# Small steps of the mixer wait in the planner for free PSUM buffers; z products share the stream's two buffers

## The chip, the cores and the metric

The kernel runs on one core of a Trainium2 chip. The metric is the device time of one execution in microseconds (us); less is better. Before the change three runs took 814.40, 811.92 and 809.09 us, a median of 811.92 us.

## What is computed

The reference is two transformer blocks in float32 on 256 tokens of width 1024. Cut to what matters here:

```
x = first_block(x)                      # attention + convolutional FFN + RMSNorm
h = layer_norm(concat([meta(16 tokens), x]))        # 272 tokens
proj = h @ w_in                         # dn q,k,v | dn z | b,a | sb q,k,v | gates
q,k,v = silu(conv4(dn_qkv)); q,k normalised;  beta, g from b, a
o_dn = gated_delta_rule(q,k,v,beta,g)   # chunks of 16, 128, 128 tokens; needs (I + A)^-1 per chunk
o_dn = rms_norm(o_dn) * silu(dn_z)
o_sb = stick_breaking_attention(sq, sk, sv)         # 8 heads
mix  = (gate0 * (o_dn @ w_branch_dn) + gate1 * (o_sb @ w_branch_sb)) @ w_out
h = layer_norm(ALPHA*h + mix);  h = layer_norm(ALPHA*h + mixture_of_32_experts(h))
```

The change lies in the mixer, the part between the first layer norm and `mix`.

## The kernel before

**The stream.** All products with large weights form one list, the stream, in a fixed order. A weight slab comes by DMA into a ring of three, ScalarE rounds a part of it (`high`, the tiles hiA and hiB) and VectorE takes the remainder (`lower`, loA and loB), so that a float32 product is three fast products. A unit of the stream is half a tile of 128 output columns, 12 products; two units fill one PSUM tile (`fm_tile`), and after the second one `emit` reads the tile. In the mixer the order is sk, dn k, v, q, sq (queries of the stick-breaking heads), sv, z (the argument of silu(dn_z)), the eight gate tiles of branch 0, then the branch products `br`, which may start only when the whole mixer is done (gate "br0", opened behind `drive(... "o2" in done and "sb3" in done)`).

**The threads.** All other work is in generators. `dn_prep` makes, for each of three chunks, the decay matrix (tile drow), the Gram matrices (gram, kq) and transposed v and q (vtp, qtp). `inverse_thread` inverts I + A by doubling: six levels, each a product Y, copies to SBUF, products Z and ZT, and subtractions; the first level is the tile xt, the last joins two halves (YL, ZL). `state_thread` then carries the state through the chunks (KS, w, Su, QS, PW), and `o_thread` normalises, transposes (otp) and writes `od`. Beside that `sb_pair` runs four pairs of heads: scores (two tiles sz), a masked add on VectorE, exponentials on ScalarE, running sums on VectorE, transposes (swm, swt), the product with the values (sav) and two reads of it into `os`.

**The order of the work.** The instructions of each engine run in the order in which the program issues them; `drive` fixes that order when the program is built. It keeps a modelled clock for each engine (`Queue`, `TensorQueue`, `Clock`), takes a thread step when its time has come, and feeds stream products when TensorE has had too few columns lately (`owed`, 1300 wanted in the mixer) or when no thread is ready. `Clock.run` lets TensorE's modelled clock run on when a step has to wait for a buffer, but the step is issued at that place all the same.

**PSUM.** It has eight buffers of 128x512 float32: four with the tag acc, two g and two a. Stream tiles take g, but the four z tiles take acc before the change; most thread steps take acc; svt, sz, swm and sav take a. A thread step takes its buffer (`acc_tile`, `a_tile`) and issues its products at once; if that buffer is still to be read by VectorE or ScalarE, TensorE stands at these products, and all that was issued behind them stands too.

`z_emit` holds its tile long: it reads it with the first exponential on ScalarE and again with a multiplication on VectorE after two more ScalarE steps:

```
A.activation(z, p, AF.Exp, scale=-1.0)
A.activation(z, z, AF.Ln, bias=1.0)
A.activation(z, z, AF.Exp, scale=-1.0)
V.tensor_mul(z, z, p)
```

Of the kernel before, what the change touches and what calls it, by code (L numbers as in the profile page):

```python
# [20 lines left out]
N_META = 16  # L21
# [26 lines left out]
WANT = 1000.0  # L48
MIX_WANT = 1300.0

TURN = 0.13
LNS = 1.0


# [8 lines left out]
class Clock:  # L63
# [49 lines left out]
    def turn(self, tag, bufs, tile):  # L113

        names = self.tags.setdefault(tag, [])
        if len(names) == bufs:
            old = min(names, key=lambda n: self.last.get(n, 0))
            names.remove(old)
            self.used[tile.name] = [((0, 128, 0, 1 << 20), at, by) for _, at, by in self.used.get(old, ())]
        names.append(tile.name)  # L120
        return tile


# [64 lines left out]
class TensorQueue:  # L188
# [23 lines left out]
    def matmul(self, out, w, x, pair=False, **k):  # L212

        n, m, r = size(x), size(w), x.shape[0]
        if x.dtype == F32:
            half = 2 if pair or (r <= 64 and m <= 64) else 1
            self.run(max(n, m) / 600 / half + 0.01, 2 * n * r / 128 / half, [out], [w, x])
        else:
            self.run(n / 2400 + (0.0115 if x.dtype == F32R else 0.0025), n * r / 128, [out], [w, x])
        return self.engine.matmul(out, w, x, **k)  # L220
# [119 lines left out]
def build(tc, I, out):  # L340
# [35 lines left out]
    with ExitStack() as ctx:  # L376
# [30 lines left out]

        def a_tile(name):
            return clock.turn("a", 2, ps.tile([128, 512], F32, tag="a", bufs=2, name=name))


        def rsqrt(v, n, rows=128):
# [17 lines left out]
        def finish(flag):  # L430
            done[flag] = clock.end
# [583 lines left out]
        def win_tiles(c0, n0, emit, name, gate=None, room=None, mk=g_tile):  # L1015
            sl_ = load_cols(win, c0, name)
            for c in range(2):
                fm_tile(sl_, c, XH, mk, n0, lambda p, c=c: emit(c, p), (gate, None), room=room)
# [40 lines left out]
        def sv_emit(f, p):  # L1059
            n = d2_turns.take()  # L1060
            sv = M["d2"]("sv")[:, :3].rearrange("p a b -> p (a b)")[:, :NT]
            A.copy(sv, p)

            def turn():
                yield
                p = a_tile("svt")
                T.transpose(p[:16, 0:128], sv[:, 0:16], ident)
                T.transpose(p[:, 128:256], sv[:, 16:144], ident)
                T.transpose(p[:, 256:384], sv[:, 144:272], ident)
                d2_turns.give(n)  # L1070
                V.tensor_copy(M["svm"][:, f * 128:f * 128 + 128], p[:16, 0:128])
                V.tensor_copy(M["svt"][:, :, f * 128:f * 128 + 128], p[:, 128:384].rearrange("p (a b) -> p a b", a=2))
                finish("sv%d" % f)

            spawn(turn())

        def z_emit(f, p):
            z = M["z"][:, f]
# [4 lines that stand above are left out]
            finish("z%d" % f)  # L1083
# [38 lines left out]
        for s in range(2):  # L1122
            win_tiles(3080 + s * 256, 0, lambda c, p, s=s: sv_emit(2 * s + c, p), "wsv", None, d2_turns.free)
        for s in range(2):
            win_tiles(1536 + s * 256, N_META, lambda c, p, s=s: z_emit(2 * s + c, p), "wz", "mix2", None, acc_tile)
        br = {}

        def merge(f, m, n):
# [421 lines left out]
        def dn_prep_thread():  # L1550

            p = acc_tile("dcp")
            for ci, (t0, C) in enumerate(CH):
                T.matmul(p[:C, ci * 4:ci * 4 + 4], ut[:C, :C], gg[:C, ci], start=True, stop=True)
            V.memset(FN, 1.0)
            V.tensor_copy(fd[:16, 0], p[:16, 0:4])
            V.tensor_copy(fd[:, 1:3], p[:, 4:12].rearrange("p (c h) -> p c h", c=2))
            yield from wait("k")
            for ci, (t0, C) in enumerate(CH):
                X_ = DNC[ci]  # L1560
                yield from room(d2_turns)
                n = d2_turns.take()
                sq = d2("dsq")
                pk = acc_tile("ktp")
                for h in range(4):
                    T.transpose(pk[:C, h * 128:(h + 1) * 128], kdT[:, h, t0:t0 + C], ident)
                if ci < 2:
                    X_["ktok"] = (dm if ci else iv).tile([128 if ci else 16, 4, 128], F32, name="ktok%d" % ci)
                for h in range(4):
                    A.activation(sq[:C, h], v4(pk)[:C, h], AF.Square, accum_out=fk[:C, ci, h:h + 1])  # L1570
                if ci < 2:
                    A.copy(X_["ktok"][:C], v4(pk)[:C])
                yield
                d2_turns.give(n)
                yield
            for n in "vq":
                yield from wait(n)
            A.preload_act_table_set("natural_log_exp_and_others")
            A.activation(fe, fd, AF.Exp)
            V.tensor_scalar(fk, fk, 1e-6, None, op0=OP.add)  # L1580
            V.reciprocal(fb_, fk)
            V.tensor_mul(fb_, fb_, beta)
            V.tensor_scalar(fn_, fe, -1.0, None, op0=OP.mult)
            rk = rsqrt_log(fk.rearrange("p c h -> p (c h)"), 12)
            V.tensor_mul(fk, fk, rk.rearrange("p (c h) -> p c h", c=3))
            for ci in (1, 2, 0):
                spawn(dn_prep(ci))
            spawn(inverse_thread())
            spawn(state_thread())
            yield  # L1590

        def dn_prep(ci):
# [4 lines left out]
            yield from room(d2_turns)  # L1597
            nE = d2_turns.take()
            E = d2("E")[:, :, :C]
            pr = acc_tile("drow")  # L1600
            for h in range(4):
                T.transpose(pr[:, h * C:(h + 1) * C], fd[:C, ci, h:h + 1].to_broadcast([C, 128]), ident[:C, :C])
# [4 lines left out]
            yield  # L1607
            A.activation(E[:C], E[:C], AF.Exp)
            yield
            p = acc_tile("gram")  # L1610
            for h in range(4):
                T.matmul(p[:C, h * C:(h + 1) * C], kdT[:, h, sl], kdT[:, h, sl], start=True, stop=True)
# [15 lines left out]
                    V.scalar_tensor_tensor(X_["PT"][:C, h], p2[:C, h * C:(h + 1) * C], fb_[:C, ci, h:h + 1], E[:C, h], op0=OP.mult, op1=OP.mult)  # L1628
            d2_turns.give(nE)
            yield  # L1630
            pv = acc_tile("vtp")
            for h in range(4):
                T.transpose(pv[:C, h * 128:(h + 1) * 128], M["raw3"][2][:, h, sl], ident)
# [47 lines left out]
        def inverse_thread():  # L1681
# [8 lines left out]
            for g in B:  # L1690
                g.mask(0)
            yield
            P = []
            for g in B:
                P.append(g.psum("xt"))
# [4 lines left out]
                V.tensor_sub(g.x, g.bc(identc), p)  # L1700
            yield
            for l in range(1, 6):
                P = []
                for g in B:
                    P.append(g.psum("Y"))
                    g.each(P[-1], g.am, lambda b, i, g=g: g.x[b, i])
                for g, p in zip(B, P):
# [5 lines left out]
                    if l < g.levels - 1:  # L1713
                        g.mask(l + 1)
                yield
                P = []
                for g in B:
                    if g.n == 8:
# [17 lines left out]
                    finish("inv0")  # L1736
                yield
            g = B[0]
            p = g.psum("YL")
            for i in range(8):  # L1740
                T.matmul(p[hi, i], DNC[1 + i // 4]["AT"][lo, i % 4, hi], g.x[lo, i], start=True, stop=True)
            A.copy(g.y[hi, 0:4], p[hi, 0:4])
            V.tensor_copy(g.y[hi, 4:8], p[hi, 4:8])
            yield
            p = g.psum("ZL")
            for i in range(8):
                T.matmul(p[lo, i], g.y[hi, i], XT[hi, i // 4, i % 4, hi], start=True, stop=True)
# [6 lines left out]
        def state_thread():  # L1754
            Sst = None
            for ci, (t0, C) in enumerate(CH):
# [4 lines left out]
                if Sst is None:  # L1761
                    R = X_["vp"]
                else:
                    yield from room(d2_turns)
                    nR = d2_turns.take()
                    R = d2("R")
                    p = acc_tile("KS")
                    for h in range(4):
                        T.matmul(p[:C, h * 128:(h + 1) * 128], kdT[:, h, sl], Sst[:, h], start=True, stop=True)
                    for h in range(4):  # L1770
                        V.scalar_tensor_tensor(R[:C, h], p[:C, h * 128:(h + 1) * 128], fn_[:C, ci, h:h + 1], X_["vp"][:C, h],
                                               op0=OP.mult, op1=OP.add)
                    yield
                yield from room(d2_turns)
                nw = d2_turns.take()
                w = d2("w")
                p = acc_tile("w")
                for h in range(4):
                    T.matmul(p[:C, h * 128:(h + 1) * 128], X_["XT"][:C, h], R[:C, h], start=True, stop=True)
# [5 lines left out]
                Sold = Sst  # L1785
                yield
                if ci < 2:
                    p = acc_tile("Su")
                    for h in range(4):
                        T.matmul(p[:, h * 128:(h + 1) * 128], X_["ktok"][:C, h], w[:C, h], start=True, stop=True)  # L1790
# [9 lines left out]
                    Sst = Sn  # L1800
                if ci > 0:
                    qs = X_["vp"]
                    p = acc_tile("QS")
                    for h in range(4):
                        T.matmul(p[:, h * 128:(h + 1) * 128], qdT[:, h, sl], Sold[:, h], start=True, stop=True)
# [30 lines left out]
        def o_thread(ci, qs, so_):  # L1836
# [5 lines left out]
            for n in range(4):  # L1842
                yield from wait("z%d" % n)
            og = qs
            p = acc_tile("otp")
            for h in range(4):
                T.transpose(p[:, h * 128:(h + 1) * 128], qs[:, h], ident)
# [21 lines left out]
        def sb_pair(pr):  # L1869
# [3 lines left out]
            nl = l_turns.take()  # L1873
            z = sw.tile([128, 2, 416], F32, "z", "z%d" % (nz % 2))
            l = sw.tile([128, 2, 416], F32, "l", "l")
            P = [a_tile("sz") for hh in range(2)]
            for a in range(2):
                for hh in range(2):
# [19 lines left out]
            yield  # L1898
            yield from room(w_turns, pr)
            nw = w_turns.take()  # L1900
            pm = a_tile("swm")
            PT = []
            for hh in range(2):
# [10 lines left out]
            V.tensor_copy(wm, pm[:16])  # L1914
            z_turns.give(nz)
            yield
            av = a_tile("sav")
            for c in range(3):
                for hh in range(2):
# [8 lines left out]
            w_turns.give(nw)  # L1928
            oh, ol = M["o"][1]
            A.copy(oh[:, pr], av[:, :S])  # L1930
            yield
            V.tensor_sub(ol[:, pr], av[:, :S], oh[:, pr].bitcast(F32))
            finish("sb%d" % pr)

        stream.open("win")
# [599 lines left out]
```

## Time and profile before

| | |
|---|---|
| median of 3 runs | 811.92 us |
| profiled execution | 807.77 us, span 806.0 us |
| TensorE matmuls busy | 764.5 us (95%) |
| VectorE busy | 503.7 us (62%) |
| ScalarE busy | 399.4 us (50%) |
| mean granted TensorE clock | 0.974 |
| DMA | 187.15 MB, mean 232 GB/s |

Times in rows are microseconds from the start of the span. PE is TensorE (PEld its weight loads), DVE VectorE, ACT ScalarE, POOL GpSimd. A busy PE says that some product was under way, not that it ran at full rate: the granted clock (PEclk) stands beside it, 1.00 for 2.4 GHz and 0.50 for 1.2 GHz, and a value between is a mean over both. The name before the arrow is the tile written, those behind it the tiles read; some small tiles are cut out of one large one and all are called cut. In brackets stands the idle time before an instruction and what ended it.

### The profile page before, as it was taken

Reading aid. Unit: us, or ns where it says so; the run is one execution under the profiler, and the core shown is the slowest. Engines: PE = TensorE matmul, PEld = TensorE weight load, DVE = VectorE, ACT = ScalarE, POOL = GpSimd, SP = SyncE. Lnnn points to the kernel's source line nnn. Section 1 sums busy time; section 2 is a strip of 40 time slices with the busy share of each in tenths; the row PEclk is TensorE's granted clock in tenths of the full one; section 3 lists DMA queues with packets and bytes.
Section 4 is the critical chain, followed back from the end, with each engine's and each line's share of the span. In section 5 each row is a group of like instructions: output and inputs, shape, how many; then the busy total and the mean of one; then the engine's idle time right before and its main releaser. Section 6 shows DMA issues by size and latency. Waiting matters only on the chain. (4 is left out here: it accounts for less than half of the span.)

```text
span 806.0 us, 17077 instructions
## 1 busy us (share of the span) xinstructions
PE 764.5 (95%) x6839; PEld 650.9 (81%) x6839; DVE 503.7 (62%) x1268; ACT 399.4 (50%) x861; POOL 46.8 (6%) x74
## 2 busy tenths in 40 slices
PE   8999999999999999999899889999999999998984
PEld 7989998999999999889898679999876555545442
DVE  6786667997888888899878638655663211130104
ACT  7555566775566666676535455745343111212201
POOL 0000001000000000343000000001300000000001
PEclk9999999999999999999999979999999999988998
DMA  8534553465455464385511104996789999999992
GB/s 299 184 110 153 164 160 105 159 216 202 158 179 188 158 207 158 106 305 166 157 54 55 54 1 157 387 403 241 267 326 365 420 425 426 420 426 423 424 390 88
DMA packets 93971, 187.15 MB, mean 232 GB/s; under 512 B 10490, under 2 KB 71219, under 8 KB 82499
## 3 DMA queue, kind: packets, MB, share of 16 engines
q1 hardware_dynamic: 93731, 185.78, 62.8%
q8 instruction: 54, 0.88, 0.4%
q10 hardware_dynamic: 160, 0.27, 0.1%
q14 instruction: 26, 0.21, 0.1%
HBM read 184.99 MB, written 1.05 MB: 231 GB/s over the span
## 5 line engine op out<-in xcount | busy, mean ns | idle before, releaser
L220 PE MATMUL fm<-ah,hiB 128*128 128x256 f32 x268 | 76.5, 286 | 0.0
L220 PE MATMUL fm<-al,hiB 128*128 128x256 f32 x268 | 75.6, 282 | 0.0
L220 PE MATMUL fm<-ah,loB 128*128 128x256 f32 x268 | 75.2, 281 | 0.0
L183 DVE TENSOR_TENSOR hd<-small,ph 128x256 f32<-128x256 f32 x8 | 3.4, 422 | 114.5 <-ACT small L183 114.5
L220 PE MATMUL fm<-ah,hiA 128*128 128x256 f32 x212 | 61.2, 289 | 0.2 <-ACT hiA L183 0.2
L220 PE MATMUL fm<-ah,loA 128*128 128x256 f32 x212 | 60.6, 286 | 0.5 <-DVE loA L183 0.5
L220 PE MATMUL fm<-al,hiA 128*128 128x256 f32 x212 | 60.5, 286 | 0.0
L220 PE MATMUL fm<-hTh,hiB 128*128 128x256 f32 (+1 forms) x184 | 56.5, 307 | 2.8 <-DVE cv L183 1.4
L220 PE MATMUL fm<-hTl,hiB 128*128 128x256 f32 (+1 forms) x184 | 53.2, 289 | 0.0
L220 PE MATMUL fm<-hTh,loB 128*128 128x256 f32 (+1 forms) x184 | 53.2, 289 | 0.0
L220 PEld LDWEIGHTS fm<-ah,hiB 128*128 128x128 f32 x268 | 50.5, 189 | 1.5 <-issue 1.3
L183 ACT ACTIVATE small<-ph 128x256 f32<-128x256 f32 x8 | 3.1, 383 | 96.0 <-PE ph L220 96.0
L220 PEld LDWEIGHTS fm<-al,hiB 128*128 128x128 f32 x268 | 50.5, 188 | 0.1
L220 PEld LDWEIGHTS fm<-ah,loB 128*128 128x128 f32 x268 | 50.5, 188 | 0.0
L183 DVE SCALAR_TENSOR_TENSOR c<-u,pc,c 128x256 f32<-128x256 f32 x88 | 42.5, 483 | 1.6
L220 PEld LDWEIGHTS fm<-ah,hiA 128*128 128x128 f32 x212 | 41.1, 194 | 1.7 <-ACT hiA L183 1.0
L220 PEld LDWEIGHTS fm<-ah,loA 128*128 128x128 f32 x212 | 41.2, 194 | 0.7 <-DVE loA L183 0.7
L220 PEld LDWEIGHTS fm<-al,hiA 128*128 128x128 f32 x212 | 41.1, 194 | 0.0
L220 PE MATMUL ph<-xg,xe 128*32 128x256 f32 x448 | 39.7, 416 | 1.4 <-DMA xg<-in_expert_w_gate_dram 1.4
L220 PEld LDWEIGHTS fm<-hTh,hiB 128*128 128x128 f32 x184 | 35.7, 194 | 6.4 <-issue 3.0
L220 PE MATMUL fm<-hTh,hiA 128*128 128x256 f32 (+1 forms) x136 | 40.4, 297 | 0.1
L220 PE MATMUL fm<-hTh,loA 128*128 128x256 f32 (+1 forms) x136 | 38.6, 284 | 0.0
(556 smaller groups left out, 2325.2 us busy)
## 6 DMA issues: line engine op xcount, KB each, us to landing
xg<-in_expert_w_gate_dram SPq DMA_DIRECT2D x24, 1024.0 KB, 19.6
xd<-in_expert_w_down_dram SPq DMA_DIRECT2D x18, 1024.0 KB, 19.7
xu<-in_expert_w_up_dram SPq DMA_DIRECT2D x16, 1024.0 KB, 14.5
cut<-in_expert_w_up_dram SPq DMA_DIRECT2D x15, 1024.0 KB, 12.4
wg<-in_ffn_w_up_dram SPq DMA_DIRECT2D x11, 1024.0 KB, 5.8
wu<-in_ffn_w_up_dram SPq DMA_DIRECT2D x11, 1024.0 KB, 5.0
wdn<-in_ffn_w_down_dram SPq DMA_DIRECT2D x11, 1024.0 KB, 5.0
wgt<-in_w_in_dram SPq DMA_DIRECT2D x8, 1024.0 KB
```

Source lines behind the costliest of these rows:

```text
L183: return f(*args, **k)
L220: return self.engine.matmul(out, w, x, **k)
```

## The change

A generator `places(tag, n)` is put ahead of the steps that take n buffers of a tag: it yields, in modelled time, until the n buffers that would be taken next have been read, or 0.1 us at a time while one of them is in `kept`. `kept` holds a sav tile between its first and second read. Meanwhile `drive` issues other threads or the stream. `Clock.turn` counts a buffer that is just taken as used last. The z tiles take g, as the rest of the stream. Two constants of the model change: 0.16 us in place of 0.13 for each turn between float32 and rounded products, and small float32 products count as at least 30 columns.

```diff
-TURN = 0.13
+TURN = 0.16
...
         names.append(tile.name)
+        self.n += 1
+        self.last[tile.name] = self.n
         return tile
...
-            self.run(max(n, m) / 600 / half + 0.01, 2 * n * r / 128 / half, [out], [w, x])
+            self.run(max(n, m, 30) / 600 / half + 0.01, 2 * n * r / 128 / half, [out], [w, x])
...
+        kept = set()
+
+        def places(tag, n=1):
+
+            bufs = {"acc": 4, "g": 2, "a": 2}[tag]
+            while True:
+                names = sorted(clock.tags.get(tag, []), key=lambda x: clock.last.get(x, 0))
+                old = names[:max(0, n - bufs + len(names))]
+                t = max((at for x in old for _, at, _ in clock.used.get(x, ())), default=0.0) + HOP
+                if kept.intersection(old):
+                    yield 0.1
+                elif t <= T.now:
+                    return
+                else:
+                    yield t - T.now
...
-            win_tiles(1536 + s * 256, N_META, lambda c, p, s=s: z_emit(2 * s + c, p), "wz", "mix2", None, acc_tile)
+            win_tiles(1536 + s * 256, N_META, lambda c, p, s=s: z_emit(2 * s + c, p), "wz", "mix2")
...
+            yield from places("acc", 2)
             p = acc_tile("gram")
...
+            yield from places("acc", 2)
             pv = acc_tile("vtp")
...
+                yield from places("acc", len(B))          # ahead of Y
...
+                yield from places("acc", len(B) + 1)      # ahead of Z and ZT
...
+            yield from places("a", 2)
             P = [a_tile("sz") for hh in range(2)]
...
+            yield from places("a")
+            yield from places("acc", 2)
             pm = a_tile("swm")
...
+            yield from places("a")
             av = a_tile("sav")
...
             A.copy(oh[:, pr], av[:, :S])
+            kept.add(av.name)
             yield
             V.tensor_sub(ol[:, pr], av[:, :S], oh[:, pr].bitcast(F32))
+            kept.remove(av.name)
```

The same line stands ahead of svt (one a), ktp, drow, xt (two acc), YL, ZL, KS, w, Su, QS with PW (two acc) and otp.

## Rows read from the trace of the kernel before

**Rows 1.** Stretches of the mixer: busy time of each engine, clock, DMA

```profile
core 0: us, PE busy (x) PEld busy (x) DVE busy (x) ACT busy (x) POOL busy (x), PEclk, DMA share, GB/s
399.00:408.00 9.00, 6.28 (x45) 5.71 (x43) 8.62 (x29) 3.11 (x18) 2.07 (x2) 0.81 0.21 76
408.00:442.00 34.00, 34.00 (x578) 29.86 (x578) 25.79 (x58) 15.07 (x30) 0.00 (x0) 1.00 0.21 64
442.00:482.00 40.00, 33.88 (x346) 27.33 (x346) 20.28 (x36) 17.53 (x34) 0.00 (x0) 0.83 0.09 28
482.00:519.00 37.00, 37.00 (x318) 36.03 (x318) 27.77 (x70) 25.51 (x64) 0.00 (x0) 1.00 0.65 240
```

**Rows 2.** Who TensorE waited for, 399 to 482: total, times, longest

```profile
PE sav L220 <- DVE cut L183: 3.3, 1, 3.3
PE sz L220 <- DVE os L183: 2.4, 1, 2.4
PE qtp L225 <- DVE cut L183: 2.0, 1, 2.0
PE vtp L225 <- DVE PT L183: 0.7, 1, 0.7
PE Y L220 <- DVE zv L183: 0.4, 1, 0.4
```

**Rows 3.** Timeline of TensorE around the three long waits: start, duration

```profile
402.80 1.09 PE L225 MATMUL qtp<-ident,qdT 128*128 128x128 f32 x4 [1.98 <-DVE cut L183]
...
446.17 0.65 PE L220 MATMUL sav<-rt,cut 16*64 16x256 f32 x4 [3.30 <-DVE cut L183]
...
449.55 1.54 PE L220 MATMUL Z<-cut 64*64 64x64 f32 x32
...
467.94 1.72 PE L220 MATMUL sz<-cut 64*128 64x144 f32 x6 [2.41 <-DVE os L183]
...
471.17 1.97 PE L220 MATMUL YL<-cut 64*64 64x64 f32 x16
```

**Rows 4.** Stretches right behind the three waits, columns as in rows 1

```profile
402.80:404.96 2.16, 2.16 (x10) 2.16 (x11) 2.15 (x10) 0.98 (x8) 0.00 (x0) 0.50 0.00 0
446.17:449.30 3.13, 3.13 (x18) 2.16 (x18) 1.04 (x2) 0.37 (x1) 0.00 (x0) 0.64 0.00 0
467.94:473.00 5.06, 5.05 (x28) 4.08 (x28) 1.09 (x2) 0.26 (x1) 0.00 (x0) 0.50 0.00 0
473.00:478.30 5.30, 5.30 (x35) 4.55 (x33) 1.80 (x3) 2.85 (x6) 0.00 (x0) 0.55 0.00 0
```

**Rows 5.** Timeline of VectorE: running sums, then the adds that free sz

```profile
441.91 2.04 DVE L183 TENSOR_TENSOR_SCAN cut<-ones,cut 128x144 f32<-128x144 f32 x4
...
445.53 1.08 DVE L183 TENSOR_TENSOR cut<-sz,smask 128x416 f32<-128x416 f32 x2
```

**Rows 6.** Timelines of TensorE and VectorE: state chain and first branch product

```profile
481.38 1.05 PE L220 MATMUL KS<-S,kdT 128*128 128x128 f32 x8
...
514.73 0.68 DVE L183 TENSOR_TENSOR od<-vp,od 128x512 fp32r<-128x512 f32 x1
...
518.58 0.46 PE L220 MATMUL br<-od,hiA 128*128 128x256 f32 x2
```

**Rows 7.** Timelines of ScalarE and VectorE: first and last z tile

```profile
454.51 0.38 ACT L183 ACTIVATE zv<-fm 128x256 f32<-128x256 f32 x1 [0.53 <-PE fm L220]
...
455.82 0.42 DVE L183 TENSOR_TENSOR zv<-zv,fm 128x256 f32<-128x256 f32 x1 [2.72 <-ACT zv L183]
...
485.31 0.39 ACT L183 ACTIVATE zv<-fm 128x256 f32<-128x256 f32 x1 [0.91 <-PE fm L220]
...
489.87 0.41 DVE L183 TENSOR_TENSOR zv<-zv,fm 128x256 f32<-128x256 f32 x1
```

**Rows 8.** Two stretches behind the mixer, columns as in rows 1

```profile
560.00:570.00 10.00, 9.62 (x73) 8.91 (x72) 10.00 (x17) 5.92 (x12) 6.41 (x6) 1.00 0.43 126
...
640.00:650.00 10.00, 10.00 (x104) 4.19 (x96) 3.59 (x19) 1.93 (x4) 0.00 (x0) 1.00 1.01 424
```

More of the change, by code (lines that the diff above doesn't have):

```diff
@@ L1563, in dn_prep_thread @@
                 sq = d2("dsq")
+                yield from places("acc")
                 pk = acc_tile("ktp")
@@ L1599, in dn_prep @@
             E = d2("E")[:, :, :C]
+            yield from places("acc")
             pr = acc_tile("drow")
@@ L1738, in inverse_thread @@
             g = B[0]
+            yield from places("acc")
             p = g.psum("YL")
@@ L1744, in inverse_thread @@
             yield
+            yield from places("acc")
             p = g.psum("ZL")
@@ L1766, in state_thread @@
                     R = d2("R")
+                    yield from places("acc")
                     p = acc_tile("KS")
@@ L1776, in state_thread @@
                 w = d2("w")
+                yield from places("acc")
                 p = acc_tile("w")
@@ L1787, in state_thread @@
                 if ci < 2:
+                    yield from places("acc")
                     p = acc_tile("Su")
@@ L1802, in state_thread @@
                     qs = X_["vp"]
+                    yield from places("acc", 2)
                     p = acc_tile("QS")
@@ L1844, in o_thread @@
             og = qs
+            yield from places("acc")
             p = acc_tile("otp")
@@ L1900, in sb_pair @@
             nw = w_turns.take()
+            yield from places("a")
+            yield from places("acc", 2)
             pm = a_tile("swm")
@@ L1916, in sb_pair @@
             yield
+            yield from places("a")
             av = a_tile("sav")
```

## The prediction

> **What bounds the kernel now.** I read the stretches of the mixer first, then TensorE's waits in it, then the timelines around the long ones. In the stretches [rows 1] one looks for a stage in which TensorE is neither full nor at full clock. It is full and at 1.00 from 408 to 442 and from 482 to 519. Between these, from 442 to 482, it is busy 33.9 of 40 us at a mean clock of 0.83, and from 399 to 408 it is busy 6.3 of 9 us at 0.81. VectorE is the fullest other engine, 8.6 of 9 us in the first of the two bad stretches but only 20.3 of 40 us in the second, where nothing but TensorE's own order explains the loss. The waits [rows 2] are five and sum to 0.7 + 2.0 + 3.3 + 0.4 + 2.4 = 8.8 us. All five are for VectorE and stand at products of thread steps that take an acc or a buffer.
>
> The timelines show that they are waits for a buffer, not for data. sav stands until 446.17 [rows 3] because the two a buffers still hold scores; the adds that read them start at 445.53 [rows 5], in VectorE's queue behind the four running sums of the pair before. Other work was at hand: Z of the inverse was issued behind sav and began at 449.55 [rows 3]. The second half of sz at 467.94 stands until os, the second read of sav, is done; YL is queued behind it. qtp at 402.80 stands for a Gram buffer.
>
> Each of the three long waits is followed by a low clock [rows 4]. It was 1.00 up to 442 [rows 1], and 0.50 (1.2 GHz) in the 2.16 us from 402.80 and in the 5.06 us from 467.94. What these stretches lose against full clock is (1 - clock) x time: 1.1 + 1.1 + 2.5 + 2.4 = 7.1 us. Between 408 and 442 the same alternation of thin thread steps and stream products ran at 1.00 [rows 1], so thin steps alone don't lower it there; the idle before does.
>
> **The change part by part.**
>
> *The waits move from TensorE's queue into the planner.* A step is now issued only when the planner holds its buffers for read, so the 8.8 us of idle can go, and with them the 7.1 us of low clock: 15.9 us at most. What fills the gaps are other thread steps (Z, YL) or stream products. The stream has some at each of the three places: stream tiles run right before and after each wait, and behind 482 it fills most of 37 us [rows 1]. Their weights are on chip or cheap to fetch: the DMA engines are 9 to 21% busy from 399 to 482 [rows 1], so ring loads that SP now issues earlier pass nothing.
>
> *But the stream is finite.* Branch products start only when od is complete. In the profile od ends at 514.73 + 0.68 = 515.4 and br starts at 518.58 [rows 6]: the gates last 3.2 us longer than the chain. From KS at 481.38 to the end of od the chain takes 34.0 us, most of it VectorE and ScalarE steps between few products. If the gaps are filled by thread steps, KS moves forward by all 15.9 us, od ends at 499.5, TensorE's work lasts until 502.7, and the gain is 15.9 us. If they are all filled by stream products, KS moves only by the clock's 7.1 us, od ends at 508.3, TensorE has run dry at 502.7, and the gain is 518.6 - 508.3 = 10.3 us less a low clock after 5.6 us of idle. That costs between 1.1 and 4.9 us, the least and the most that one wait was followed by [rows 4] (4.9 is the sum of its last two). So the bounds are 5.4 and 15.9 us. The two long waits behind 442 had thread steps queued right behind them, the first one had not, so I take the middle of 10.3 and 15.9, 13.1 us.
>
> *z in the stream's buffers.* A z tile is held from ScalarE's first read to the end of VectorE's multiplication: 455.82 + 0.42 - 454.51 = 1.7 us for the first, 489.87 + 0.41 - 485.31 = 5.0 us for the last, whose multiplication was queued behind other VectorE work [rows 7]. With two buffers the next tile but one needs it. One tile is 24 products at 37.00 / 318 = 0.116 us [rows 1], 2.8 us, and thread steps in between lengthen that. A hold of 1.7 us costs nothing; one of 5.0 us costs up to 2.2 us, and behind the waiting product stand all thread steps. Bounds: 0, and four tiles at 2.2 us, 8.8 us. I take one tile, 2.2 us, since one of the two that I read has the long hold. On the other side the inverse gets the whole of acc; no wait in the rows is for a z tile in acc, so this is 0.
>
> *Longer waits of single steps.* A thread that waits resumes only between stream groups, and Z with ZT now wants up to three of four acc buffers free at once. The steps are queued behind a full TensorE, which covers this; if it didn't, it would be a share of the chain bound above.
>
> *The two constants and the bookkeeping in turn* change no instruction, but they shift the order in every stage with threads. No row shows such a shift; TensorE is full before and behind the bad stretches, which leaves little to win. I take 0, with bounds of 2.8 us either way, the distance from the median to the lowest run, below which nothing could be told.
>
> *Behind the mixer.* The last stage is bound by DMA, 1.01 busy at 424 GB/s from 640 to 650, but at 560 to 570 DMA is only 0.43 busy [rows 8]: loads wait there for buffers that computation frees, so the whole tail moves with the mixer. I take the gain in full; its lower bound is nothing of it, if the weights set the end by themselves.
>
> Sum: 13.1 - 2.2 = 10.9 us. The profiled execution, 807.77 us, becomes 796.9. The median of the runs is 4.15 us above that execution, so I predict 801 us.
>
> **The rivals.** A measurement of this kernel can tell 1%, 8.1 us, from no change: faster means below 803.8, slower above 820.0.
>
> (a) The forecast: the long waits go, the chain keeps up in part; 796 to 803.5 us. Chance 0.60.
>
> (b) The state chain takes over. The gaps are filled by stream products alone, TensorE runs dry ahead of od and its clock falls: 811.9 - 5.4 = 806.5 us. For it speaks that the planner prefers stream products whenever few columns ran lately; against it that Z and YL stood ready. Chance 0.19.
>
> (c) The change does not do what it says: the planner believes the buffers read earlier than VectorE reads them, and TensorE stands as before, or stands elsewhere as long; 812 us. Against it: the planner charges 2.0 us for the four running sums (0.07 us each and 2/960 us a column), and the row has 2.04 [rows 5]. Chance 0.11.
>
> (d) z's multiplication becomes the wait, and the result is slower. Squeezed into fewer microseconds VectorE is fuller, each of the four z tiles is held 5.0 us like the last one, each costs 2.2 us, and each such wait is followed by the longest low clock, 4.9 us: 4 x 7.1 = 28.4 us against 15.9 saved, 824 us. It decides against the kernel from 6 us a tile on (4 x 6 = 24.0 = 15.9 + 8.1), a hold of 3.9 us if the clock falls as far each time. Against it: the first tile's 1.7 us, and thread steps between the tiles. Chance 0.10.
>
> The Trainium skill ("TensorE: Matmul & The Clock Gate", section "A second HAM failure mode: psum-queue depth-cycling") describes (d) in kind: a kernel that cycled through its PSUM banks left TensorE micro-idle between groups of products, and the clock swung between its two levels. By that rule two buffers in place of four would bring the clock down in the z tiles; the trace of before, with z in four, can't show it.
>
> **How the numbers follow.** The likeliest case gives 801 us. The low end is the whole 15.9 us and the 2.8 us of the lowest run: 811.9 - 18.7 = 793. The high end is case (c) with a little spread, 813. Left out are (d) and the worst of (c). Faster by over 1%: (a), 0.60. Slower: (d), 0.10. Within: the rest, 0.30.
>
> **What would show it.** Right: no wait over 1 us at vtp, qtp, sav or sz, a clock of 1.00 through the mixer, the first br near 508 us in place of 518.58 [rows 6], and the expert stage as long as before. (b) would show as idle of TensorE right ahead of br, and gates finished before od; (c) as the same releasers in TensorE's waits; (d) as waits of fm for zv. A mixer shorter by ten us without a shorter run would refute the step on the tail. Wrong altogether would be a gain that comes from another stage.

## The result, and the profile after

The changed kernel took 799.61 us, the median of four runs (798.24 to 801.28), against 810.50 us before (four runs, 807.10 to 814.40): a ratio of 0.987, interval 0.9842 to 0.9897. That is 10.9 us less, the size that was forecast; how much of this agreement is luck is told below. Measured once more it took 798.45 us against 809.40, ratio 0.9858 (0.9840 to 0.9876). The profile shown is that of the first measurement; its execution took 801.28 us, the slowest of its four, with a span of 799.5 us.

The stretches of the mixer answer to [rows 1], with the same columns; the last one ends where the branch products begin:

```profile
399.00:408.00 9.00, 7.18 (x55) 6.80 (x54) 8.72 (x32) 3.08 (x13) 1.78 (x2) 0.83 0.37 117
408.00:442.00 34.00, 33.03 (x572) 29.14 (x572) 25.84 (x57) 12.67 (x32) 0.29 (x1) 0.99 0.15 45
442.00:482.00 40.00, 39.63 (x445) 33.93 (x446) 29.13 (x60) 25.70 (x49) 0.00 (x0) 1.00 0.22 70
482.00:509.70 27.70, 27.15 (x232) 26.05 (x231) 21.86 (x53) 18.13 (x50) 0.00 (x0) 1.00 0.53 188
```

The stretch from 442 to 482 is the one to look at: TensorE is busy 39.6 us in place of 33.9 and runs at 1.00 in place of 0.83. VectorE is busy 29.1 us in place of 20.3: the products that feed it come earlier, so more of its work falls into this stretch. From 399 to 408 little is better.

The waits of TensorE from 380 to 510 answer to [rows 2]:

```profile
PE qtp L227 <- DVE cut L185: 1.8, 1, 1.8
PE Y L222 <- DVE cut L185: 0.6, 1, 0.6
PE swm L227 <- ACT cut L185: 0.6, 1, 0.6
PE fm L222 <- DVE cv L185: 0.5, 1, 0.5
PE xt L222 <- DVE cut L185: 0.4, 1, 0.4
PE swm L227 <- DVE cut L185: 0.3, 1, 0.3
```

sav and sz are gone, qtp is not, and four small ones are new. (The wait of fm for cv lies before 399 and is there in both kernels.) What runs in their place is seen in TensorE's timeline, which answers to [rows 3, 6]:

```profile
404.77 0.92 PE L227 MATMUL qtp<-ident,qdT 128*128 128x128 f32 x4 [1.82 <-DVE cut L185]
...
441.89 1.15 PE L222 MATMUL Z<-cut 64*64 64x64 f32 x32
...
446.28 0.65 PE L222 MATMUL sav<-rt,cut 16*64 16x256 f32 x4
...
459.90 0.38 PE L222 MATMUL YL<-cut 64*64 64x64 f32 x3
...
467.48 1.05 PE L222 MATMUL KS<-S,kdT 128*128 128x128 f32 x8
...
509.73 0.41 PE L222 MATMUL br<-od,hiA 128*128 128x256 f32 x2
```

The Z that stood behind sav is now issued ahead of it, at 441.89 where it was 449.55; sav runs at the time at which it ran before, without a wait. From there the inverse is ahead: YL 11.3 us, KS 13.9 us. The branch products begin 8.9 us earlier. VectorE writes the last od here:

```profile
504.74 0.68 DVE L185 TENSOR_TENSOR od<-vp,od 128x512 fp32r<-128x512 f32 x1
```

It ends at 505.4, and gate products fill another 4.3 us to the branch products. So the state chain was not what ended the mixer.

### The profile page after: what moved, and what is told of

The parts are those of the page before. It is cut to its first block, busy times and chain, and to the rows that moved or that the text cites. A ratio compares the mean times of both kernels' runs of the same rounds, so it can differ in the third digit from the quotient of the medians.

```text
span 799.5 us, 17087 instructions
## 1 busy us (share of the span) xinstructions
PE 760.5 (95%) x6839; PEld 647.8 (81%) x6839; DVE 503.9 (63%) x1268; ACT 400.2 (50%) x862; POOL 46.6 (6%) x74
## 5 line engine op out<-in xcount | busy, mean ns | idle before, releaser
L222 PE MATMUL ph<-xg,xe 128*32 128x256 f32 x448 | 37.8, 402 | 2.9 <-DMA xg<-in_expert_w_gate_dram 2.9
L222 PE MATMUL fm<-hTl,hiA 128*128 128x256 f32 (+1 forms) x136 | 38.6, 284 | 0.0
```

## The experiments

All times are medians; a ratio is against the kernel before, run beside it on the same chip, and can differ a little from the quotient of two medians. Those of one group ran together.

**First group, to tell the three parts apart.** All planner waits taken out of the changed kernel:

```diff
         def places(tag, n=1):
+            if n:
+                return
```

> The changed kernel with every planner wait taken out again: z in the stream's buffers and the two new constants stay. Waits theory (the gain comes from the steps that are no longer issued ahead of a buffer that is still to be read): the gain is lost, about 810 us, ratio to before 0.995 to 1.005, and waits of 2 to 3 us at sav, sz and qtp are back with a clock of 0.5 behind them. Rival Z (moving z out of acc frees buffers for the inverse, and that is the gain): 800 to 803 us. Rival C (the constants shift the order to a better one): 800 to 804 us as well.

816.14 us, ratio 1.0076 (1.0047 to 1.0104). Its waits of TensorE from 408 to 510:

```profile
PE sav L222 <- DVE cut L185: 5.2, 1, 5.2
PE svt L227 <- DVE cut L185: 3.4, 1, 3.4
PE sz L222 <- DVE os L185: 3.1, 1, 3.1
```

The planner's waits are the gain, and more than it: without them the rest of the change loses 5 us where no loss was expected, with 11.7 us of idle at three steps that take an a buffer. Rivals Z and C fall.

The z tiles back in acc:

```diff
-  ..., "wz", "mix2")
+  ..., "wz", "mix2", None, acc_tile)
```

> The changed kernel with the four z tiles back in acc. Waits theory: the planner's waits do the work wherever z is, 799 to 803 us, and no wait of TensorE over 1 us at sav or sz. Rival Z: the gain goes, 806 to 811 us. The prediction's step on z (2.2 us for one long hold in two buffers): about 2 us faster than the changed kernel, 797 to 798 us, if the hold costs what was said; no difference if no product waits for a z tile.

799.55 us, ratio 0.9866 (0.9837 to 0.9895): no difference to the changed kernel. No product waits for a z tile in either.

The old constants:

```diff
-TURN = 0.16
+TURN = 0.13
...
-max(n, m, 30) / 600
+max(n, m) / 600
```

> The changed kernel with the two old constants of the model (0.13 us for a turn, no floor of 30 columns). Waits theory: 798 to 803 us, the order in the mixer shifts a little. Rival C: back to 808 to 811 us.

796.80 us, ratio 0.9818 (0.9789 to 0.9847). The new constants are not the gain; they may cost some 2 to 3 us, which the intervals, 0.9818 (to 0.9847) and 0.9858 (from 0.9840), don't separate. In this profile qtp is the only wait from 395 to 510:

```profile
PE qtp L227 <- DVE cut L185: 2.0, 1, 2.0
```

Planner waits for a buffers alone:

```diff
         def places(tag, n=1):
+            if tag == "acc":
+                return
```

> The changed kernel with planner waits for the a buffers alone (svt, sz, swm, sav); steps that take acc are issued at once as before. Waits theory, by place: sav and sz made 5.7 us of idle and, with the low clock behind them, about 11.7 us of the loss; vtp and qtp, the acc waits, made 3.8 us and the changed kernel still has the larger one. So 800 to 804 us. Rival (the acc waits are what the inverse and the state chain needed): 806 to 811 us, with YL near 470 us in place of 460.

798.84 us, ratio 0.9850 (0.9820 to 0.9880): all of the gain, and a little less time than expected. YL began at 457.0, so the inverse does not need the acc waits.

**Second group.** The changed kernel again, as the measure of this group:

> The changed kernel as it is, beside the others on one chip, as their measure: 798 to 801 us. Its profile had a low clock from 330 to 336, ahead of the mixer, that the kernels with z in acc, with the old constants and with a waits alone did not have. If that was chance, this profile is without it or has it elsewhere; if it belongs to this order of work, it is there again.

798.45 us, ratio 0.9858 (0.9840 to 0.9876). Its profile has no low clock from 320 to 340; the last section comes back to that.

Planner waits for acc buffers alone:

```diff
         def places(tag, n=1):
+            if tag == "a":
+                return
```

> The counterpart to the kernel that waits for a buffers alone: planner waits for acc only, steps that take an a buffer are issued at once. If the a waits are the whole of it, this is no faster than the kernel without any planner waits, 812 to 816 us, with waits over 2 us at sav, svt or sz. If either half suffices, because it shifts the order, 799 to 804 us.

817.88 us, ratio 1.0107 (1.0088 to 1.0126), a little above the range expected. Its three long waits from 408 to 510 are those of the kernel without any planner wait, to the tenth:

```profile
PE sav L222 <- DVE cut L185: 5.2, 1, 5.2
PE svt L227 <- DVE cut L185: 3.4, 1, 3.4
PE sz L222 <- DVE os L185: 3.1, 1, 3.1
PE xt L222 <- DVE cut L185: 0.4, 1, 0.4
```

So, with the durations that the planner now counts, the waits for acc change the time by nothing that can be measured, and the four for a do all. What the acc waits do is seen at vtp: its wait is gone in the changed kernel and 0.6 us long in the one that waits for a buffers alone.

The planner's cost of the Gram operations, with the old constants:

```diff
   V.scalar_tensor_tensor(X_["AT"][r, h, 0:C - b], ...)
+  V.now += 0.1 * full
```

> The changed kernel with the old constants, and the planner charges 0.1 us more for each of the eight VectorE operations of a chunk that read a full Gram tile (they take 2.63 us in the trace, the planner counts 1.8). Theory: the wait of qtp that the change left, 1.8 to 2.0 us, stayed because the planner believed the Gram buffer read earlier; it then goes, with the low clock behind it, and the run takes 793 to 795 us against 796.8 with the old constants alone. Rival: the step is merely late and the inverse starts later by as much, so no difference, 796 to 798 us.

794.38 us, ratio 0.9802 (0.9782 to 0.9821), the fastest kernel of this study; its interval lies below that of the changed kernel beside it. Its waits from 395 to 510:

```profile
PE xt L222 <- DVE cut L185: 1.2, 1, 1.2
PE qtp L227 <- DVE cut L185: 0.6, 1, 0.6
PE br L222 <- DVE od L185: 0.5, 1, 0.5
```

The wait of qtp shrank from 1.8 or 2.0 to 0.6 us, so the cause named for it, a planner that counts too little, is shown. Part of the idle came back at xt (1.2 us, where the changed kernel had 0.4 us in one profile and 1.7 in the other), which is the rival's case. How much of the 4.1 us against the changed kernel is the Gram cost and how much the old constants is open: against the old constants alone (0.9818, another group) the intervals overlap. The last row is new: for the first time the branch products wait for od, that is, the stream has run out 0.5 us before od is written and the state chain ends the mixer.

The smallest version, with z in acc, old constants and planner waits for a alone, as a diff from the changed kernel:

```diff
+            if tag == "acc":
+                return
...
+  ..., "wz", "mix2", None, acc_tile)
...
-TURN = 0.16
+TURN = 0.13
...
-max(n, m, 30) / 600
+max(n, m) / 600
```

> The smallest version: the kernel before with planner waits for a buffers (and the bookkeeping of taken buffers), z in acc, old constants. If the a waits are the whole of the gain: 796 to 800 us. If they need z out of acc or the acc waits beside them: 804 to 811 us.

798.67 us, ratio 0.9871 (0.9854 to 0.9887): the gain of the whole change, from the planner waits at svt, sz, swm and sav, with `kept` and the counting of taken buffers that belong to them. What these two add, and what the waits at svt and swm give, was not tried apart.

**Third group, on the smallest version and on the kernel before.** No planner wait ahead of the scores:

```diff
-            yield from places("a", 2)
             P = [a_tile("sz") for hh in range(2)]
```

> The smallest version (planner waits for a buffers alone, 798.7 us) without the wait ahead of the scores sz. If the terms of the prediction hold place by place, what the sz wait cost before comes back: 2.4 us of idle and 4.9 us of low clock behind it, 806 us. If any of the a waits shifts the order enough, 798 to 800 us; if the sav wait hits another step instead, more than 806.

797.60 us, ratio 0.9840 (0.9807 to 0.9873). Nothing came back. Its waits from 408 to 510:

```profile
PE sz L222 <- DVE rt L185: 0.4, 1, 0.4
PE sav L222 <- DVE cut L185: 0.4, 1, 0.4
```

With sav in its right place, sz, issued at once, meets buffers that are nearly free. So the terms do not add up place by place.

No planner wait ahead of sav:

```diff
-            yield from places("a")
             av = a_tile("sav")
```

> The smallest version without the wait ahead of sav. Place by place, 3.3 us of idle and 1.1 to 1.7 us of low clock come back: 803 us. If the scores' wait alone does the work, 798 to 800 us; if sav then stands longer behind the scores, up to 5.2 us as in the kernel without any planner wait, 805 us or more.

803.28 us, ratio 0.9899 (0.9856 to 0.9942), 5.7 us above the kernel without the sz wait beside it: each of its four runs (799.80 to 804.26) is slower than each of that kernel's (797.57 to 798.59), though the two intervals just overlap. The smallest version itself ran in another group, and its interval (0.9854 to 0.9887) does not separate from this one; the loss rests on the neighbour and on the trace. Its waits from 408 to 510, and its stretch from 442 to 482 with the columns of [rows 1]:

```profile
PE sav L222 <- DVE cut L185: 3.3, 1, 3.3
PE Y L222 <- DVE zv L185: 0.4, 1, 0.4
PE swm L227 <- DVE cut L185: 0.2, 1, 0.2
```

```profile
442.00:482.00 40.00, 36.08 (x405) 30.24 (x405) 24.21 (x46) 21.74 (x43) 0.00 (x0) 0.96 0.17 54
```

The old wait of sav is back to the tenth, with a clock of 0.96, 1.6 us of loss: 3.3 + 1.6 = 4.9 us of the 5.7. A planner wait at sav alone was not tried.

The new constants alone, on the kernel before:

```diff
-TURN = 0.13
+TURN = 0.16
...
-max(n, m) / 600
+max(n, m, 30) / 600
```

> The kernel before with the two new constants alone, to tell why the kernel without planner waits was 5 us slower than before. If the constants shift the order badly: 813 to 817 us, with waits of sav and svt over 3 us. If z in the stream's buffers does it: 809 to 812 us here.

815.33 us, ratio 1.0058 (1.0036 to 1.0080). From 408 to 510 the waits are others than before:

```profile
PE sz L220 <- DVE os L183: 8.1, 2, 5.1
PE svt L225 <- DVE cut L183: 3.3, 1, 3.3
PE swm L225 <- ACT cut L183: 0.6, 1, 0.6
```

The longest are at sz and svt, not at sav as expected. So the constants are what makes the kernel without planner waits slower than before: they shift the order by a little, and steps that are issued regardless meet other buffers.

z in the stream's buffers alone, on the kernel before:

```diff
-  ..., "wz", "mix2", None, acc_tile)
+  ..., "wz", "mix2")
```

> The kernel before with the z tiles in the stream's buffers alone, no planner waits, old constants. If z in two buffers costs time by itself (the step of the prediction on z, 2.2 us): 812 to 814 us, with a wait of fm for zv. If it only changes which step meets which buffer: anything from 808 to 817 us, and no fm wait for zv. If z in acc had hindered the inverse: 806 to 808 us.

809.81 us, ratio 1.0000 (0.9973 to 1.0028). Its waits are sav 3.3 and sz 2.4 us, as before, and none of fm for zv. The wait of Y for zv [rows 2] is gone; it stays in the kernel without the sav wait above, which has z in acc.

## Why the prediction was right, step by step

**What bounds the kernel** held. The idle and the low clock between 442 and 482 were TensorE's own order: with it mended VectorE did 29.1 us of work in a stretch that had held 20.3. The waits were for buffers: when the planner waits for them, those of sav, sz and vtp are gone.

**The waits move into the planner** held for three of the five (vtp, sav, sz). Y waits in both profiles, 0.4 us for zv before and 0.6 us for cut after, but that is another Y and another cause. The idle from 399 to the first branch product was 8.8 us; after, qtp 1.8, Y 0.6, swm 0.9 and xt 0.4 make 3.7. What failed is qtp: I argued from the running sums, 2.04 us against 2.0 planned, that the planner knows when VectorE reads. For the Gram buffers it does not. VectorE's timeline after shows the eight operations of one chunk:

```profile
401.99 2.63 DVE L185 SCALAR_TENSOR_TENSOR cut<-gram,FN,E 64x128 f32<-64x128 f32 x8
```

The planner counts 0.13 us and 1/960 us a column for each, 8 x 0.13 + 768 / 960 = 1.84 us, 0.79 too little. The chunk before it, at 398.09, also took 2.63 us, so my estimate is that VectorE runs some 1.6 us behind the planner at this place, most of the 1.8 that qtp waits. So rival (c) was true at this one place.

**The low clock** was priced from the pieces right behind the waits at 7.1 us. Over the whole stretches (1 - clock) x time is 9 x 0.19 + 40 x 0.17 = 8.5 us before and 9 x 0.17 + 34 x 0.01 = 1.9 us after. 5.1 us of idle and 6.6 us of clock make 11.7 us, against the 13.1 that I took.

**The stream is finite**: 13.1 us was near the 11.7 found, but for a reason that does not hold. I took the middle between gaps filled by thread steps and gaps filled by the stream. The gaps were filled by thread steps, Z and YL first; KS came 13.9 us earlier, and gates still ran 4.3 us behind od. The chain did not end the mixer; what is missing is the waits and the low clock that stayed, 3.7 and 1.9 us. The chain does come into play in the version with the Gram cost, where br waits 0.5 us for od.

**z in the stream's buffers** was mis-sized: 2.2 us forecast, no cost that can be measured, in the changed kernel and in the kernel before. The longest of the four holds after is the third: ScalarE's first read and VectorE's multiplication are

```profile
468.13 0.38 ACT L185 ACTIVATE zv<-fm 128x256 f32<-128x256 f32 x1
```

```profile
471.37 0.41 DVE L185 TENSOR_TENSOR zv<-zv,fm 128x256 f32<-128x256 f32 x1
```

3.65 us, more than one tile's 2.8 us of products, but thread steps stand between the tiles, as the prediction said and did not count. The prediction also misread [rows 2] when it said that no wait is for a z tile in acc. In the profile before, Y waits until the first z multiplication ends, 455.82 + 0.42 = 456.24 [rows 7]:

```profile
456.30 1.15 PE L220 MATMUL Y<-cut 64*64 64x64 f32 x32 [0.41 <-DVE zv L183]
```

With z alone moved out of acc this wait is gone; it is 0.4 us in favour of the move. Rival (d) needed 3.9 us four times and the longest low clock after each. The clock is 1.00 from 442 to 482, where the z tiles run: what the Trainium skill says in "TensorE: Matmul & The Clock Gate", section "A second HAM failure mode: psum-queue depth-cycling", did not happen with two buffers here. That two buffers would be too few was my own step from that section.

**The constants** were taken at 0, with 2.8 us as the bound. Alone they cost 815.33 - 810.27 = 5.1 us; under planner waits the medians differ by 2 to 3 us, which is not clear of noise, and with planner waits for a buffers alone no cost shows: 0.9850 with the new constants, 0.9871 with the old ones (and z in acc). The reason given, that full stages leave little to move, missed the mixer, where a small shift decides which buffer a step meets. So a bound of 2.8 us was too small where steps are issued regardless; whether the constants cost anything in the changed kernel stays open.

**The tail** moved with the mixer, though not quite in full. From the first branch product to the end it was 806.0 - 518.6 = 287.4 us before, 799.5 - 509.7 = 289.8 after, and 797.2 - 507.7 = 289.5 in the second profile of the changed kernel. Two new waits of 0.6 us stand right there, from 505 to 565 of the profile after:

```profile
PE fm L222 <- ACT gt L185: 0.6, 1, 0.6
PE br L222 <- DVE gt L185: 0.6, 1, 0.6
```

They are half of it; where the rest went, I don't know. Over all fourteen profiles this part takes between 286.8 and 290.5 us. The branch products were forecast near 508 us: 507.7 in that second profile, 509.7 in the one shown, which had lost 2.2 us ahead of the mixer.

**The sum.** The medians differ by the 10.9 us that were forecast, but the prediction took its terms from the profiled execution, and between the profiled executions the gain is smaller: 807.77 to 801.28 us is 6.5 us, and to the second profile (798.96 us) 8.8. The 4.15 us added for the median were scatter of the runs before; the median after lies 1.7 us below its profiled execution. Of the terms, 1.4 us forecast too much in the mixer and a tail 2.1 to 2.4 us longer stand against the 2.2 us that z did not cost; the first profile also lost 2.2 us ahead of the mixer. The direction, the place and most of the idle and low clock were foreseen; the agreement to the tenth is luck.

## What to carry to other kernels

Where one in-order engine carries a latency-bound chain and a stream of filler, a step should be issued only when its buffer is free; one step that stands holds up the steps behind it that were ready, and a low clock can follow the idle: in the kernel without the line ahead of sav a wait of 3.3 us cost 4.9. One wait can be the consequence of another, so leave them out one by one: here leaving out the line ahead of sz cost nothing, and leaving out the one ahead of sav instead made the kernel 5.7 us slower than that. A planner that decides such an order is only as good as its durations, so compare them with the trace for each kind of operation that frees a buffer, and don't take one that agrees for all.

## What was not expected of the hardware

The same program, at the same place, may or may not lose the clock. Ahead of the mixer TensorE waits about 1 us for a sum. The profile of the changed kernel, TensorE's timeline and the stretch behind it:

```profile
331.29 1.01 PE L222 MATMUL lnst<-ones,xs 128*128 128x1 f32 x4 [0.86 <-DVE xs L185]
```

```profile
330.00:335.00 5.00, 4.13 (x18) 3.81 (x18) 2.85 (x13) 0.62 (x1) 0.69 (x1) 0.50 0.90 310
335.00:340.00 5.00, 5.00 (x36) 5.00 (x35) 3.30 (x9) 3.42 (x8) 2.16 (x3) 0.83 0.01 2
```

And the second profile of the same kernel:

```profile
331.35 0.61 PE L222 MATMUL lnst<-ones,xs 128*128 128x1 f32 x4 [1.06 <-DVE xs L185]
```

```profile
320.00:340.00 20.00, 18.75 (x151) 18.31 (x151) 16.86 (x42) 12.46 (x27) 4.85 (x7) 1.00 0.33 106
```

One runs at 0.50 behind the wait, the other, with a longer wait, at 1.00; drow began at 393.0 us in the one and at 390.9 in the other. The fall was there in four of the fourteen profiles, kernels with and without planner waits among them. Behind qtp's wait of 1.82 us it is the same: 0.83 from 399 to 408 in the one, 1.00 in the other, whose stretch is

```profile
399.00:408.00 9.00, 5.65 (x49) 4.59 (x47) 8.86 (x28) 3.65 (x19) 2.07 (x2) 1.00 0.19 69
```

Not every wait is so uncertain. In six of the fourteen profiles (before, old constants, z alone, the smallest version and the two that leave out one of its lines) qtp waits 1.98 us, and the clock is 0.50 in the 3 us behind it in all six. In seven it waits 1.82 or 1.83 us, and the clock behind it is 0.53, 0.53 and 0.75 in the three that had also fallen ahead of the mixer, 1.00 in the four that had not. The two groups differ in the order of work too, so what decides it is not shown. The fall ahead of the mixer cost 393.0 - 390.9 = 2.1 us here, and since one program has it in one profile and not in another, one more such fall is no sign of a worse order.
